# Query blocks of the token mixers as a sixth Strassen group, with adding transfers in the mixers and at the heads of the FFNs

## The chip, the cores and the metric

The kernel runs on one core of one Trainium2 chip. The metric is the device time of one execution in microseconds (us); the median of several executions is compared. Engines are named as the profile names them: PE (TensorE, matmuls), DVE (VectorE), ACT (ScalarE), POOL (GpSimd) and SP (SyncE, which here only issues transfers).

## The reference

One block of a streaming encoder on a sequence of 256 frames of width 2048, all in float32:

```
x = x + 0.5 * ffn(rmsnorm(x, g1), w1g, w1u, w1d)        # ffn: (silu(x@wg) * (x@wu)) @ wd, width 5632
h = rmsnorm(x, gm)
q_a, k_a, v_a, q_r, k_r, v_r, g_r, gate_a, gate_r = split(h @ w_in)
branch_a = chunked_band_attention(q_a, k_a, v_a, rel_bias) @ w_out_att
branch_r = (silu(g_r) * retention(rotary(q_r), rotary(k_r), v_r)) @ w_out_ret
x = x + (sigmoid(gate_a) * branch_a + sigmoid(gate_r) * branch_r) @ w_out
x = x + 0.5 * ffn(rmsnorm(x, g2), w2g, w2u, w2d)
out = rmsnorm(x, gf)
```

Each of q_a, k_a, v_a, q_r, k_r, v_r and g_r is 1024 columns wide (8 heads of 128), gate_a and gate_r are 2048 wide each.

## The kernel before, in words

**Products.** A float32 product is made of three faster ones (`three`, L137 to L145): ACT rounds a weight tile to its high part (L131), DVE subtracts to get the low part (L132), and PE multiplies high by high, low activations by high weights, and high by low. A weight tile holds 256 rows by 512 columns, 512 KB.

**Steps.** All work on PE is a list of steps that the Python code lays out before anything is issued. A *standard step* (L147) multiplies one weight tile by both halves of the sequence: 12 matmuls. A *Strassen step* (L573) does 6. A Strassen group (class `Strassen`, L518) computes two blocks of 512 columns from two weight blocks with 7 products of half-size blocks instead of 8: 28 steps, where standard jobs take 2 x 8 standard steps. In return it makes sums of weight tiles. Its group number is in its tile names (z10, z392, z728: the index of its first step), followed in the name of a split tile by phase, pair and r or s.

**Phases of a group.** The weights come in four pairs of tiles, k (kept) and x. Phase 0 multiplies the k tiles (r steps) and the sums x+k (s steps); phase 1 multiplies a third block from the ring of raw tiles (r) and the sums x+third (s); phase 2 a fourth block (r) and x-k (s); phase 3 the x tiles once more, to which POOL has added a weight block by an adding transfer (L587, it issues after DVE's subtraction L586). The first sum x+k is made by DVE (`first`, L534) or, for the pairs named in `added`, by an adding transfer from SBUF to SBUF on POOL's queue (`add_on`, L547), issued `ADD_WAIT` = 6 steps after the load of x. If the k tile of an added pair is prepared before that transfer is issued, DVE does the sum after all (L594). The FFNs have `ADDED = (0, 1)`; the mixers have none.

**What sets the order.** `run` (L249) goes through the steps; before the products of step c it prepares the weight tiles up to four steps ahead (casts on ACT, subtractions on DVE), and runs whatever is due at step c (`later`, `at`). Each engine works its own instructions in that order. SP loads raw tiles into a ring of 5, as the ring comes free. POOL loads the k and x tiles (`loads`, L540) into a room of 8 (`KEPT`); the first group's loads are spread over the 8 steps ahead of it (L712), one a step, and the FFNs get room for 2 more (`EXTRA`) when the first group has ended (L730). POOL also runs the norms' roots, loads the relative bias and reads back the gates, and it too works in order: a transfer that waits for another to land holds up what stands behind it.

**Weaving.** `weave` (L688) first lays out `lead` standard steps, then all groups one after the other, and lets in standard steps between their parts by a credit that grows with `share`. A group of an FFN has 8 standard steps among its 28, one of the mixers 9.6 on average.

**The stages.** FFN1: one plain block of columns and ten groups. Mixers: the standard jobs QA, KA, VA (two blocks each) and the first block of VR are woven with five groups (the two gates, in four blocks each, and g_r), whose results ACT writes to DRAM (L1056). At step `mixed` the woven part ends. Then come VR's second block, the jobs QR and KR, the three output products, and FFN2. The attention's heads (L916) and the retention's run beside these jobs: head h starts 4 steps after `mixed` plus 4h (L978, L1213), its scores, softmax, transposes and values spread over 6 steps. The query and key blocks are turned by PE into tiles of the pool `act` (`to_transposed`, L845), which has 30 tiles of 512 KB, 16 of them taken by the normalized activations in the mixers.

**Start.** Nine matmuls on zeros (L1170, `WARM`) run before the first product, 6 and 3.

Of the kernel before, what the change touches and what calls it, by code (L numbers as in the profile page):

```python
# [8 lines left out]
F32 = mybir.dt.float32  # L9
# [6 lines left out]
P = 128  # L16
SEQ = 256
# [9 lines left out]
NB = 512  # L27
# [10 lines left out]
AHEAD = (2, 3)  # L38
HALF_K = D // P // 2
LEAD = (10, 8)  # L40
MIX_LEAD = 8
RET_WAIT = (14, 5)
HELD = 6

MIX_SHARE = (0.85,) * 4 + (1.0,) * 4 + (0.8,) + (0.4,) * 3 + (0.15,) * 4
SHARE = (0.75,) * 4 + (1.0,) * 4 + (0.0,) * 4 + (0.2,) * 4
ADDED = (0, 1)
ADD_WAIT = 6
# [1 line left out]
PASSES = ((10,),) + tuple((b,) for b in range(10))  # L50
GATE_WAIT = 16
SQUARES = 8
WARM = (6, 3)
TAIL_PARTS = ((0, slice(0, NB)), (1, slice(0, NB // 2)), (1, slice(NB // 2, NB)))


# [21 lines left out]
def block_kernel(ctx: ExitStack, tc: tile.TileContext, x, g1, w1g, w1u, w1d, gm, w_in, rel, woa, wor, wo,  # L78
# [439 lines left out]
    class Strassen:  # L518
# [3 lines left out]

        def __init__(self, norm, w1, col1, w2, col2, evict, added=()):
            self.added, self.summed = added, set()
            self.norm, self.w, self.col, self.evict = norm, (w1, w2), (col1, col2), evict
            self.x, self.kept, self.acc, self.wide = {}, {}, {}, {}
            self.name = f"z{len(steps)}"
# [12 lines left out]
        def loads(self):  # L540


            def go(tiles, i, jc):
                tiles[jc] = apool.tile([P, KC, NB], F32, tag="act", name=f"{self.name}{'kx'[i]}{jc}")
                nc.gpsimd.dma_start(tiles[jc], chunk(self.w[i], self.rows(0, jc), self.col[i]))

            def add_on(jc):  # L547
                if jc not in self.summed:
                    self.summed.add(jc)
                    nc.gpsimd.dma_start(self.x[jc], self.kept[jc], accum_op=ALU.add)  # L550

            def second(jc):
                go(self.x, 1, jc)
                if jc in self.added:
                    later(ADD_WAIT, lambda: add_on(jc))

            return [
                (lambda jc=jc: second(jc)) if i else (lambda jc=jc: go(self.kept, 0, jc))
                for jc in range(HALF_K // KC) for i in range(2)
            ]  # L560
# [12 lines left out]
        def step(self, phase, jc, of_sum):  # L573
            made = {}
            name = f"{self.name}{phase}{jc}{'rs'[of_sum]}"
            n = HALF_K // KC

            def load():
                made["raw"] = weights_tile(f"raw{name}")
                i = 2 - phase  # L580
                fetch(made["raw"], self.w[i], self.rows(1, jc), self.col[i])

            def third():

                x, k = self.x[jc], self.kept[jc]
                nc.vector.tensor_sub(k, x, k)  # L586
                nc.gpsimd.dma_start(x, chunk(self.w[0], self.rows(1, jc), self.col[0]), accum_op=ALU.add)  # L587

            def prep():
                x = self.x[jc]  # L590
                if not of_sum:
                    if phase == 0:
                        made["w"] = split(self.kept[jc], name)
                        if jc not in self.summed:  # L594
                            self.summed.add(jc)
                            self.first(jc)
                        return
                    raw = made.pop("raw")
                    made["w"] = split(raw, name)
                    if phase == 1:  # L600
                        nc.vector.tensor_add(x, x, raw)
                elif phase == 2:
                    made["w"] = split(self.kept.pop(jc), name)
                elif phase == 3:
                    made["w"] = split(self.x.pop(jc), name)
                else:
                    made["w"] = split(x, name)
                    if phase == 1:
                        third()

            bank, form, fresh, closing = {
# [4 lines left out]
            }[phase, of_sum]  # L616

            def products():
                hi, lo = made["w"]
                if fresh and jc == 0:  # L620
                    self.bank(bank)
                three([
                    (
                        self.acc[bank], self.norm.form(form, KC * jc + i), (hi[:, i, :], lo[:, i, :]),
                        fresh and jc == 0 and i == 0, closing and jc == n - 1 and i == KC - 1,
                    )
                    for i in range(KC)
                ], True)
# [59 lines left out]
    def weave(jobs, apart, groups, lead, share, start=None, extra=0):  # L688
# [17 lines left out]

        for _ in range(lead):
            next_standard()
        ends = []
        rate = (len(queue) - apart) / (len(groups) * sum(share))  # L710
        credit = 0.0
        first = max(len(steps) - 8, D // NB)  # L712
        for n, (b, make) in enumerate(groups.items()):
            group = make()
            loads = group.loads()
            if start is not None and n == 0:
                loads[0] = lambda load=loads[0]: [start(), load()]
            kept.extend((first + i if n == 0 else 0, fn) for i, fn in enumerate(loads))
            for i, part in enumerate(group.steps()):
                steps.extend(part)  # L720
                credit += rate * share[i]
                if i + 1 == len(share):
                    at_hand[b] = len(steps) + 7

                turn = i + 1 == 3 * (HALF_K // KC)
                if (turn or credit >= (0.2 if (i + 1) % (HALF_K // KC) == 0 else 0.6)) and next_standard():
                    credit -= 1
            ends.append(len(steps))
        if extra:
            due.setdefault(ends[0], []).append(lambda: room.update(kept=room["kept"] + extra))  # L730
            due.setdefault(ends[-1], []).append(lambda: room.update(kept=room["kept"] - extra))
        for job, k in queue:
            steps.append(standard(job, k))

# [103 lines left out]
    QA, KA, VA, QR, KR, VR, GR, GA, GG = 0, W, 2 * W, 3 * W, 4 * W, 5 * W, 6 * W, 7 * W, 7 * W + D  # L838
    scale = HD ** -0.5
    tposed, nat = {}, {}  # L840

    def heads_t(ts):
        return slice(ts * P, (ts + 1) * P)

    def to_transposed(key, b, srcs, steps):  # L845

        dst = act_tile(F32, f"{key}{b}T")
        tposed[key, b] = dst

        def go(t):  # L850
            ps = transpose4(srcs[t], f"{key}{b}p{t}").rearrange("p (i q) -> p i q", i=4)
            if t == 0:
                nc.scalar.copy(dst[:, :, heads_t(t)], ps)
            else:
                nc.vector.tensor_copy(dst[:, :, heads_t(t)], ps)

        for t in range(NT):
            later(steps[t], lambda t=t: go(t))

    def att_qk_done(key, b):  # L860
        def done(acc):
# [40 lines left out]
    def nat_done(key, b, func, after=None):  # L902
        def done(acc):
            dst = act_tile(F32, f"{key}{b}")
            nat[key, b] = dst.rearrange("p a q -> p (a q)").rearrange("p (t n) -> p t n", t=NT)
            for t in range(NT):
                nc.scalar.activation(nat[key, b][:, t, :], acc[t], func, scale=nm.scale(t))
            if after is not None:
                after()

        return done
# [63 lines left out]
    def all_attention():  # L975
        for h in range(HEADS):
            for s, stage in attention(h):
                later(2 + 4 * h + s, stage)  # L978

    def retention(b):  # L980

# [65 lines left out]
    def gates(col1, col2, func, dsts):  # L1047
# [7 lines left out]
                nc.scalar.activation(r, bank, func, scale=nm.scale(t))  # L1055
            nc.scalar.dma_start(dsts[side][:, t, :], r)  # L1056

        return Strassen(nm, w_in0, col1, w_in0, col2, evict)

    both = ("acc", "acc")  # L1060
    groups = {
        b: (lambda b=b: gates(GA + b * NB, GG + b * NB, AF.Sigmoid, merge_dram[b])) for b in range(D // NB)
    }
    groups["gr"] = lambda: gates(GR, GR + NB, AF.Silu, ret_dram)
    weave(
        [proj(QA + b * NB, att_qk_done("qa", b), both) for b in range(2)]
        + [proj(KA + b * NB, att_qk_done("ka", b), both) for b in range(2)]
        + [proj(VA + b * NB, nat_done("va", b, AF.Copy), both) for b in range(2)]
        + [proj(VR, nat_done("vr", 0, AF.Copy), both)],
        0, groups, MIX_LEAD, MIX_SHARE,  # L1070
    )
    mixed = len(steps)
    add([proj(VR + NB, nat_done("vr", 1, AF.Copy))])
    for b in range(2):
        add([proj(QR + b * NB, ret_qk_done("qr", b)), proj(KR + b * NB, ret_qk_done("kr", b, lambda b=b: retention(b)))])

# [133 lines left out]
    at(mix - 18, load_rel)  # L1210
    at(mix - 18, lambda: later(4, load_gain(gm, 1)))
    at(mixed - 4, set_bias)
    at(mixed + 2, all_attention)  # L1213
    at(merges[0][0] + 4, lambda: later(8, load_gain(g2, 2)))
    at(mixed + 16, load_ret_gates)
    at(mixed + 20, set_decay)
# [66 lines left out]
```

## Time and profile before

| | us |
|---|---|
| median of 3 runs | 2058.67 (2058.22 to 2059.67) |
| the profiled execution | 2059.72 |
| its span, first to last instruction | 2058.0 |
| PE busy | 2039.3 (99%) |
| DVE busy | 1769.2 (86%) |
| ACT busy | 1490.3 (72%) |
| POOL busy | 327.1 (16%) |

The stages in this span: FFN1 to about 697, the woven part of the mixers to 1045, the rest of the mixers to about 1350, FFN2 to the end. A timeline row gives the start, the duration, the engine, the line, the operation, and output <- inputs; what stands in brackets is the engine's idle time ahead of it and what ended that. A row of the transfers gives the queue that issued them, their count, their size and the time from issue to landing. In a row of windows stand the stretch, its length, the busy time of PE, PEld, DVE, ACT and POOL, the granted clock, the share of the transfer engines, and GB/s. A busy PE isn't proof of full pace, as its matmuls overlap; the distance of starts shows that.

### The profile page before, as it was taken

The page shows a single profiled execution, that of the slowest core. Times are in us where ns is not written, and L with a number is a line of the kernel's source. Part 1 is how long each engine was busy: PE and PEld are TensorE (multiplying, and loading weights), DVE is VectorE, ACT ScalarE, POOL GpSimd, SP SyncE. Part 2 cuts the span into 40 slices and gives each one's busy share as a digit, 9 for nine tenths or more (in the row PEclk, how much of TensorE's full clock was granted, in tenths as well). Part 3 has the DMA queues.
Part 4 walks back from the last instruction along what each step waited for, and adds up shares of the span by engine and source line. Part 5 has one row for each costly group of instructions (what it writes and reads, how often), then busy time and mean ns, then how long its engine had stood idle before and what let it go on. Part 6 is the DMA issues. An engine that isn't in the chain of part 4 may idle for free.

```text
span 2058.0 us, 26285 instructions
## 1 busy us (share of the span) xinstructions
PE 2039.3 (99%) x9208; PEld 1683.2 (82%) x9208; DVE 1769.2 (86%) x1840; ACT 1490.3 (72%) x1894; POOL 327.1 (16%) x382
## 2 busy tenths in 40 slices
PE   9999999999999999999999999999999999999998
PEld 7688888888888888888888888888788888888886
DVE  7999999999998799889966667569989999989996
ACT  7778887888788767776665434556788787888785
POOL 1221222211112110122100000011112221112200
PEclk9999999999999999999999999999999999999999
DMA  8888899888878677788775645576889988889973
GB/s 288 242 241 265 259 273 277 258 238 251 263 231 264 239 206 253 255 283 263 216 274 177 222 141 190 185 243 192 260 265 267 275 241 237 267 260 274 276 205 133
DMA packets 224629, 496.37 MB, mean 241 GB/s; under 512 B 15520, under 2 KB 16272, under 8 KB 224496
## 3 DMA queue, kind: packets, MB, share of 16 engines
q1 hardware_dynamic: 156736, 301.50, 43.6%
q0 software_dynamic: 64416, 187.35, 35.0%
q10 hardware_dynamic: 3344, 5.84, 0.8%
q8 instruction: 72, 1.18, 0.2%
q14 instruction: 61, 0.50, 0.1%
HBM read 466.84 MB, written 8.91 MB: 231 GB/s over the span
## 4 chain that ended last, share of the span: by engine, by line
PE 92%; DVE 2%; DMA 1%; ACT 1%; issue 1%; POOL 0%; DVEq 0%; POOLq 0%; ACTq 0%
PE acc L145 15%; PE acc L142 15%; PE acc L143 15%; DMA z728x<-in_ffn_w_gate_dram 1%; DMA z728x<-z728k 1%; DVE lo L132 1%; PE z765a L142 0%; PE z154a L142 0%; PE z226a L142 0%; PE z946a L143 0%; PE z873a L142 0%; PE z298a L143 0%; PE z118a L143 0%; PE z801a L145 0%; PE z982a L145 0%
## 5 line engine op out<-in xcount | busy, mean ns | idle before, releaser
L132 DVE TENSOR_TENSOR lo<-raw,hi 128x1024 fp32r<-128x1024 f32 x367 | 446.2, 1219 | 140.2 <-ACT hi L131 138.5
L131 ACT CAST hi<-raw 128x1024 fp32r<-128x1024 f32 x367 | 383.8, 1050 | 174.6 <-PE acc L143 137.9
L805 ACT ACTIVATE xall<-acc 128x512 f32<-128x512 f32 x160 | 94.3, 589 | 13.6 <-PE acc L145 9.7
L802 ACT ACTIVATE acc<-xall 128x512 f32<-128x512 f32 x160 | 95.8, 599 | 9.1 <-DVE f1g L769 4.9
L142 PE MATMUL acc<-hi,mgh 128*128 128x512 f32 x128 | 50.2, 392 | 0.0
L143 PE MATMUL acc<-hi,mgl 128*128 128x512 f32 x128 | 49.8, 389 | 0.0
L142 PE MATMUL acc<-hi,nma01h 128*128 128x512 f32 x96 | 38.7, 404 | 0.0
L142 PE MATMUL acc<-hi,nma00h 128*128 128x512 f32 x96 | 38.6, 402 | 0.0
L143 PE MATMUL acc<-hi,nma01l 128*128 128x512 f32 x96 | 37.5, 390 | 0.0
L143 PE MATMUL acc<-hi,nma00l 128*128 128x512 f32 x96 | 37.4, 390 | 0.0
L143 PE MATMUL acc<-hi,nma11l 128*128 128x512 f32 x96 | 37.4, 390 | 0.0
L142 PE MATMUL acc<-hi,nma10h 128*128 128x512 f32 x96 | 37.4, 390 | 0.0
L142 PE MATMUL acc<-hi,nma11h 128*128 128x512 f32 x96 | 37.4, 390 | 0.0
L143 PE MATMUL acc<-hi,nma10l 128*128 128x512 f32 x96 | 37.4, 390 | 0.0
L145 PE MATMUL acc<-lo,mgh 128*128 128x512 f32 x128 | 35.5, 389 | 0.0
L145 PE MATMUL acc<-lo,nma01h 128*128 128x512 f32 x96 | 29.6, 390 | 0.0
L145 PE MATMUL acc<-lo,nma11h 128*128 128x512 f32 x96 | 29.6, 389 | 0.0
L145 PE MATMUL acc<-lo,nma00h 128*128 128x512 f32 x96 | 29.6, 389 | 0.0
L145 PE MATMUL acc<-lo,nma10h 128*128 128x512 f32 x96 | 29.6, 389 | 0.0
L145 PEld LDWEIGHTS acc<-lo,mgh 128*128 128x128 f32 x128 | 24.0, 188 | 5.0
L143 PEld LDWEIGHTS acc<-hi,mgl 128*128 128x128 f32 x128 | 24.0, 188 | 4.9
L142 PEld LDWEIGHTS acc<-hi,mgh 128*128 128x128 f32 x128 | 24.0, 188 | 4.8
(6633 smaller groups left out, 7111.7 us busy)
## 6 DMA issues: line engine op xcount, KB each, us to landing
raw<-in_ffn_w_down_dram SPq DMA_DIRECT2D x176, 512.0 KB, 7.0
raw<-in_w_in_dram SPq DMA_DIRECT2D x96, 512.0 KB, 4.7
raw<-in_w_out_dram SPq DMA_DIRECT2D x32, 512.0 KB, 4.1
raw<-in_ffn_w_up_dram SPq DMA_DIRECT2D x16, 512.0 KB, 5.5
raw<-in_w_out_att_dram SPq DMA_DIRECT2D x16, 512.0 KB, 4.3
raw<-in_w_out_ret_dram SPq DMA_DIRECT2D x16, 512.0 KB, 4.3
raw<-in_ffn_w_gate_dram SPq DMA_DIRECT2D x15, 512.0 KB, 4.8
z392x<-in_w_in_dram POOLq DMA_DIRECT2D x8, 512.0 KB, 7.5
```

Of the source, the lines that this page charges most:

```text
L131: nc.scalar.copy(hi, raw)
L132: nc.vector.tensor_sub(lo, raw, hi.bitcast(F32))
L142: nc.tensor.matmul(acc, ahi, whi, start=first, stop=False, **more)
L143: nc.tensor.matmul(acc, alo, whi, start=False, stop=False, **more)
L145: nc.tensor.matmul(acc, ahi, wlo, start=False, stop=last, **more)
L802: nc.scalar.activation(acc, xs[t][:, cols], AF.Copy, scale=2.0)
L805: nc.scalar.activation(xs[t][:, cols], acc, AF.Copy, scale=0.5)
```

## The change

- The two query blocks QA leave the standard jobs and become the first Strassen group of the mixers, `qa`. VR's second block joins the woven jobs, so `mixed` is followed at once by QR. There are now six groups with 7 standard steps each, after a lead of 6.
- The mixers' groups get adding transfers for pairs 0 and 2, and room for 2 more k or x tiles. The first group of each woven stage (FFN1, mixers, FFN2) gets adding transfers for all four pairs, issued 2 steps after the load of x. An added pair's sum falls back to DVE only when its s step is prepared, not its r step.
- The 2 more tiles of room come in phase 1 of the first group, and are taken back when the last has ended.
- Query, key and value tiles of the attention are written to DRAM by ACT's queue as soon as they are made, and read back by POOL's near `mixed`: block 0 from 3 steps ahead of it, block 1 from 5 steps behind it.
- The heads start at steps 3, 6, 10, 13, 17, 20, 24 and 27 after `mixed`.
- One warm-up matmul less.

```diff
-MIX_LEAD = 8
+MIX_LEAD = 6
+MIX_ADDED = (0, 2)
+HEAD_AT = (3, 6, 10, 13, 17, 20, 24, 27)
-MIX_SHARE = (0.85,) * 4 + (1.0,) * 4 + (0.8,) + (0.4,) * 3 + (0.15,) * 4
+MIX_SHARE = (0.5,) * 4 + (1.0,) * 4 + (0.0,) * 4 + (0.2,) * 4
-WARM = (6, 3)
+WARM = (6, 2)
...
             self.added, self.summed = added, set()
+            self.add_wait = ADD_WAIT
...
-                    later(ADD_WAIT, lambda: add_on(jc))
+                    later(self.add_wait, lambda: add_on(jc))
...
                         made["w"] = split(self.kept[jc], name)
-                        if jc not in self.summed:
+                        if jc not in self.added:
                             self.summed.add(jc)
                             self.first(jc)
                         return
...
                 else:
+                    if phase == 0 and jc not in self.summed:
+                        self.summed.add(jc)
+                        self.first(jc)
                     made["w"] = split(x, name)
...
             group = make()
+            if n == 0 and group.added:
+                group.added, group.add_wait = tuple(range(HALF_K // KC)), 2
...
             for i, part in enumerate(group.steps()):
+                if i == HALF_K // KC + 2:
+                    seconds.append(len(steps))
...
-            due.setdefault(ends[0], []).append(lambda: room.update(kept=room["kept"] + extra))
-            due.setdefault(ends[-1], []).append(lambda: room.update(kept=room["kept"] - extra))
+            due.setdefault(seconds[0], []).append(lambda: room.update(kept=room["kept"] + extra))
+            due.setdefault(len(steps), []).append(lambda: room.update(kept=room["kept"] - extra))
...
+    to_dram = {key: [dram.tile([P, 4, SEQ], F32, name=f"{key}{b}d") for b in range(HEADS // 4)] for key in ("qa", "ka", "va")}
+
+    def put_away(table, key, b, tile):
+        nc.scalar.dma_start(to_dram[key][b], tile)
+        del table[key, b]
+
+    def bring_back(b):
+        for table, key in ((tposed, "qa"), (tposed, "ka"), (nat, "va")):
+            t = act_tile(F32, f"{key}{b}back")
+            nc.gpsimd.dma_start(t, to_dram[key][b])
+            table[key, b] = t if table is tposed else by_tokens(t)
...
+        if home is not None:
+            later(max(steps) + 1, lambda: put_away(tposed, key, b, dst))
...
-                later(2 + 4 * h + s, stage)
+                later(HEAD_AT[h] + s, stage)
...
-        return Strassen(nm, w_in0, col1, w_in0, col2, evict)
+        return Strassen(nm, w_in0, col1, w_in0, col2, evict, MIX_ADDED)
...
+    def queries():
+        srcs = [{}, {}]
+
+        def evict(t, side, r):
+            if side == 0:
+                bank, r = r, tmp_tile(f"qa0{t}", "gate", 2)
+                nc.scalar.activation(r, bank, AF.Copy, scale=nm.scale(t))
+            srcs[side][t] = r
+            if len(srcs[side]) == NT:
+                to_transposed("qa", side, srcs[side], (3, 3))
+
+        return Strassen(nm, w_in0, QA, w_in0, QA + NB, evict, MIX_ADDED)
+
+    groups = {"qa": queries, **groups}
     weave(
-        [proj(QA + b * NB, att_qk_done("qa", b), both) for b in range(2)]
-        + [proj(KA + b * NB, att_qk_done("ka", b), both) for b in range(2)]
+        [proj(KA + b * NB, att_qk_done("ka", b), both) for b in range(2)]
         + [proj(VA + b * NB, nat_done("va", b, AF.Copy), both) for b in range(2)]
-        + [proj(VR, nat_done("vr", 0, AF.Copy), both)],
-        0, groups, MIX_LEAD, MIX_SHARE,
+        + [proj(VR + b * NB, nat_done("vr", b, AF.Copy), both) for b in range(2)],
+        0, groups, MIX_LEAD, MIX_SHARE, None, EXTRA,
     )
     mixed = len(steps)
-    add([proj(VR + NB, nat_done("vr", 1, AF.Copy))])
...
-    at(mixed + 2, all_attention)
+    at(mixed - 3, lambda: bring_back(0))
+    at(mixed + 5, lambda: bring_back(1))
+    at(mixed, all_attention)
```

More of the change, by code (lines that the diff above doesn't have):

```diff
@@ L708, in weave @@
             next_standard()
-        ends = []
+        seconds = []
         rate = (len(queue) - apart) / (len(groups) * sum(share))
@@ L727, in weave @@
                     credit -= 1
-            ends.append(len(steps))
         if extra:
-            due.setdefault(ends[0], []).append(lambda: room.update(kept=room["kept"] + extra))
-            due.setdefault(ends[-1], []).append(lambda: room.update(kept=room["kept"] - extra))
+            due.setdefault(seconds[0], []).append(lambda: room.update(kept=room["kept"] + extra))
+            due.setdefault(len(steps), []).append(lambda: room.update(kept=room["kept"] - extra))
         for job, k in queue:
@@ L840, in block_kernel, with by_tokens @@
     tposed, nat = {}, {}
+    to_dram = {key: [dram.tile([P, 4, SEQ], F32, name=f"{key}{b}d") for b in range(HEADS // 4)] for key in ("qa", "ka", "va")}
[7 more added lines that the diff above has]
+            table[key, b] = t if table is tposed else by_tokens(t)
+    def by_tokens(t):
+        return t.rearrange("p a q -> p (a q)").rearrange("p (t n) -> p t n", t=NT)
     def heads_t(ts):
@@ L848, in to_transposed @@
         tposed[key, b] = dst
+        home = to_dram.get(key)
         def go(t):
@@ L904, in done @@
             dst = act_tile(F32, f"{key}{b}")
-            nat[key, b] = dst.rearrange("p a q -> p (a q)").rearrange("p (t n) -> p t n", t=NT)
+            nat[key, b] = by_tokens(dst)
             for t in range(NT):
                 nc.scalar.activation(nat[key, b][:, t, :], acc[t], func, scale=nm.scale(t))
+            if key in to_dram:
+                put_away(nat, key, b, dst)
             if after is not None:
```

## The prediction

> **What bounds the kernel now.** I read the page first, then TensorE's waits, then its timeline at the starts of the three stages, then the software queue.
>
> ```profile
> span 2058.0 us, 26285 instructions
> PE 2039.3 (99%) x9208; PEld 1683.2 (82%) x9208; DVE 1769.2 (86%) x1840; ACT 1490.3 (72%) x1894; POOL 327.1 (16%) x382
> ```
>
> The profiled execution took 2059.7 us: a span of 2058.0 and 1.7 around it. TensorE is busy for 99% of it, so a change can gain in two ways only: fewer matmuls, or fewer of the few waits that TensorE still has. Who ends those waits:
>
> ```profile
> PE z728c L142 <- ACT hiz72800s L131: 1.4, 1, 1.4
> PE z10c L145 <- DVE loz1003s L132: 1.2, 1, 1.2
> PE f2a0p L387 <- DVE z692c L785: 0.7, 1, 0.7
> PE kr0p L387 <- DVE attl L382: 0.6, 1, 0.6
> ```
>
> Two groups stand out: z10, the first Strassen group of FFN1, and z728, the second of FFN2. Nothing of the mixers' woven part is among the long ones. The pace of an undisturbed step comes from three neighbouring starts in the timeline of PE:
>
> ```profile
> 1427.55 0.39 PE L142 MATMUL z692a<-hiz69213s,n2s6h 128*128 128x512 f32 x1
> 1428.90 0.39 PE L142 MATMUL acc<-hi,n2a01h 128*128 128x512 f32 x1
> 1431.62 0.39 PE L142 MATMUL z692b<-hiz69220r,n2a01h 128*128 128x512 f32 x1
> ```
>
> A Strassen step (6 matmuls) takes 1.36 us and a standard step (12) 2.72, 0.227 a matmul. (The 0.39 of one matmul is its latency.) With these I can say what the two groups lose:
>
> ```profile
> 39.34 0.39 PE L142 MATMUL z10a<-hiz1000r,n1a00h 128*128 128x512 f32 x1
> 107.09 0.39 PE L142 MATMUL z46a<-hiz4600r,n1a00h 128*128 128x512 f32 x1
> 1451.56 0.39 PE L142 MATMUL z728a<-hiz72800r,n2a00h 128*128 128x512 f32 x1
> 1468.52 0.40 PE L142 MATMUL z728c<-hiz72802s,n2s5h 128*128 128x512 f32 x1
> ```
>
> z10 takes 107.09 - 39.34 = 67.75. In it lie 28 Strassen steps (38.1), 8 standard ones (21.8) and one set of eight transposes (some 0.9): 60.8. So about 7.0 is lost. From 1451.56 to 1468.52 are 16.96, with six Strassen steps, one standard step and eight transposes: 11.8. About 5.2 is lost.
>
> **The change, part by part.** *Query blocks as a Strassen group.* Two jobs of 8 standard steps go (16 x 2.72 = 43.5) and 28 Strassen steps come (28 x 1.36 = 38.1): **-5.4**, all of it on TensorE's path. The transposes of the queries stay. VR1 only moves into the woven part.
>
> *One warm-up matmul less.*
>
> ```profile
> 8.41 0.63 PE L142 MATMUL acc<-hi,n1a00h 128*128 128x512 f32 x1
> 8.84 0.63 PE L143 MATMUL acc<-hi,n1a00l 128*128 128x512 f32 x1
> ```
>
> Starts are still 0.43 apart here, at the slow clock. If the clock rises at a fixed time, one more real matmul is done before that, worth 0.23 later: **-0.2** (0 to -0.4).
>
> *FFN1's first group.* VectorE did all four first sums; now four adding transfers do.
>
> ```profile
> L534 DVE TENSOR_TENSOR z10x<-z10x,z10k 128x1024 f32<-128x1024 f32 x4 | 4.9, 1218 | 0.0
> 52.92 1.03 ACT L131 CAST hiz1003s<-z10x 128x1024 fp32r<-128x1024 f32 x1
> 55.46 1.22 DVE L132 TENSOR_TENSOR loz1003s<-z10x,hiz1003s 128x1024 fp32r<-128x1024 f32 x1
> ```
>
> VectorE is freed of 4.9 us, and its lag behind ScalarE (55.46 against 52.92 + 1.03, some 1.5) is what TensorE waits for. But the sums now come from GpSimd's queue. Its prices:
>
> ```profile
> 21.27 0.91 POOL L545 DMA_DIRECT2D z10k<-in_ffn_w_up_dram  x1
> 26.51 0.74 POOL L545 DMA_DIRECT2D z10x<-in_ffn_w_gate_dram  x1
> z10k<-in_ffn_w_up_dram POOLq DMA_DIRECT2D x1, 512.0 KB, 7.2
> z10x<-in_ffn_w_gate_dram POOLq DMA_DIRECT2D x1, 512.0 KB, 16.5
> 1434.13 1.18 POOL L545 DMA_DIRECT2D z728x<-in_ffn_w_gate_dram  x1
> z728x<-in_ffn_w_gate_dram POOLq DMA_DIRECT2D x1, 512.0 KB, 17.5
> 1443.96 0.93 POOL L550 DMA_DIRECT2D z728x<-z728k  x1 [8.64 <-DMA z728x<-in_ffn_w_gate_dram]
> z728x<-z728k POOLq DMA_DIRECT2D x1, 512.0 KB, 10.7
> z82x<-z82k POOLq DMA_DIRECT2D x1, 512.0 KB, 5.3
> ```
>
> The first of the eight loads lands at 28.5, the eighth at 43.0: 2.07 each, one after the other. An adding transfer behind other work lands 3.0 after its predecessor (1454.7 against 1451.6); one that finds the queue empty takes 5.3. GpSimd will issue k0 x0 k1 x1, sum 0, k2 x2, sum 1, k3 x3, sum 2, sum 3. Each sum waits on GpSimd for its x, and the later loads are queued behind it. If all eight loads and four sums go at 2.07 and 3.0, the last sum lands at 26.4 + 16.6 + 12.0 = 55.0 or a little later; if the last two pairs go faster, because the raw weights' queue is quiet in phase 0, x3 lands near 47.5 and the last sum near 53.3. ScalarE's cast of it is now at 52.92, so at 53.3 the low part is ready near 55.5 and not at 56.7: 1.2 earlier. At 55.0 it is ready at 57.3, later than now, and phase 1 starts some 0.6 to 1.0 later. Behind that, VectorE works through phase 1 as before: its sums and differences are not touched, so the later losses of z10 stay. I take **-1.2** (bounds -3.0 and +1.0), nearer to the quick end, as few raw weights are due there.
>
> *FFN2's second group.* Its loads start only at 1430.48, since room for two more tiles came at the end of group one:
>
> ```profile
> 1430.48 1.21 POOL L545 DMA_DIRECT2D z728k<-in_ffn_w_up_dram  x1
> 1454.77 1.04 ACT L131 CAST hiz72800s<-z728x 128x1024 fp32r<-128x1024 f32 x1 [3.14 <-DMA z728x<-z728k]
> ```
>
> The room now comes in phase 1 of group one, so the first pair is there long before. The second pair takes the first one's place in the queue, and its sum lands by 1454.7; without the stall its cast is due at about 1456.5. What stays is the transposes of f2a0p, which wait for VectorE (0.7 and the restart, about 1.2): **-4.0** (bounds -2.5 and -5.2). FFN2's own first group shows no wait now; four sums cost it nothing by the same queue order, and up to 1.0 if they are late.
>
> The Trainium skill (SBUF — State Buffer, section "SBUF: two separate sides") says that a transfer issued from GpSimd cannot get its descriptors written while VectorE holds the shared port in a two-port mode. The rows speak against it here: from 1430.48 to 1434.13 GpSimd issued six loads, 0.73 apart, in a stretch in which VectorE is loaded like the rest of FFN2.
>
> *The mixers' first group.*
>
> ```profile
> 702.47 0.75 POOL L545 DMA_DIRECT2D z392k<-in_w_in_dram  x1
> z392k<-in_w_in_dram POOLq DMA_DIRECT2D x1, 512.0 KB, 4.6
> 720.49 0.39 PE L142 MATMUL z392a<-hiz39200r,nma00h 128*128 128x512 f32 x1
> ```
>
> With a lead of 6 it starts two standard steps sooner, at 715.0, and its loads two steps sooner; k0 and x0 pass ahead of the norm's root on GpSimd. From k1 (landing at 702.5 + 4.6 = 707.1) five loads and four sums follow: 707.1 + 10.4 + 9.2 to 12.0 = 726.7 to 729.5. The last sum's cast is due by 726: seven Strassen steps and one standard step after 715.0 are 727.2, less the cast. **+1.0** (bounds 0 and +3.0).
>
> *The mixers' steady part.*
>
> ```profile
> 92.00:98.00 6.00, 5.45 (x22) 4.08 (x23) 5.50 (x6) 6.00 (x7) 1.07 (x2) 1.00 1.04 391
> 240.00:301.00 61.00, 61.00 (x275) 50.59 (x274) 56.77 (x53) 49.46 (x61) 12.51 (x14) 1.00 0.91 263
> 855.00:920.00 65.00, 65.00 (x292) 53.64 (x291) 57.69 (x52) 43.85 (x49) 10.66 (x12) 1.00 0.82 254
> ```
>
> A group has 28 Strassen and 7 standard steps, 57.1 us, where 9.6 standard steps made it 64.2. VectorE has 57.69 in 65 now, so 57.0 a group; less two sums and 2.6 splits at 1.22 leaves 51.4 of 57.1, 90%. FFN1 runs at 56.77 of 61, 93%, without waits. Transfers: 29 of 0.52 MB, four gate tiles of 0.26 and one tile put away make 16.8 MB in 57.1 us, 294 GB/s; the queues reach 391. The put-away waits of ScalarE for VectorE's copy hold back casts that run three steps ahead. **+0.5** (bounds 0 and +3.0).
>
> *Attention.*
>
> ```profile
> 1018.95 2.02 POOL L349 DMA_DIRECT2D biasT<-rel_ext  x2
> biasT<-rel_ext POOLq DMA_DIRECT2D x2, 512.0 KB, 13.4
> 1045.29 0.60 PE L360 MATMUL psb<-id_sb,biasT 128*128 128x128 f32 x4
> ```
>
> GpSimd issues the bias right after the last group's last third-block transfer, 26.3 before the mixers' end; in the new order 12 Strassen and 2 standard steps lie there, 21.8. The bias lands 13.4 later, three returned tiles 6.2 after it: 2 us before the end, and the first head comes three standard steps (8.2) beyond it. So 10 us cover the return; without them TensorE would wait for the tiles directly. Heads follow each other in 3.5 steps instead of 4, between transposes that already wait once (0.6): **+0.5** (bounds -0.6 and +3.0, five such waits).
>
> Sum: -5.4 - 0.2 - 1.2 - 4.0 + 1.0 + 0.5 + 0.5 = **-8.8**, or 2050.9 against the profiled execution. The median of the runs, 2058.67, lies 1.0 below that execution, so the forecast is **2049.9**. All ends together are -14.6 (2044.1) and +2.1 (2060.8).
>
> **The rivals.** *Late sums at the heads.* All adding transfers cost 3.0 and more: z10 +1.0, FFN2's first group +1.0, its second only -2.5, the mixers' head +3.0. With -5.4 and -0.2 that is -3.1 and, with the two half microseconds, -2.1: about 2056.6. For it: every busy-queue sum I could price took 3.0. Against: the loads of phase 0 meet few raw weights. [...]
>
> *More gain.* With VectorE freed at its start, z10 loses nothing further and z728's stall goes whole: -5.4 - 0.2 - 7.0 - 5.2 = -17.8, or 2040.9. Against: VectorE is unbroken through z10's phase 1, where nothing is taken away.
>
> *The sums aren't done by transfers.* Where the sum's step is prepared before its transfer is issued, VectorE does it after all. Then z10 and the mixers' head stay as now: -8.6, beside the forecast. In the order as worked out the transfers come three steps ahead, so I hold it unlikely.
>
> *Slower: raw weights late in the mixers.*
>
> ```profile
> raw<-in_w_in_dram SPq DMA_DIRECT2D x5, 512.0 KB, 16.4
> ```
>
> This is SP's queue at 761 to 772, while eight loads pass on GpSimd's. Five buffers at one raw tile per 2.72 us cover 13.6, and with fewer standard steps and two adding transfers a group, TensorE could wait 16.4 - 13.6 = 2.8 in each of five group changes: +14.0, so 2063.9. It decides as soon as a raw tile lands more than 13.6 after TensorE could have used its buffer. Against: with 16.4 TensorE shows no such wait today, and the FFNs carry the same pattern at 263 GB/s.
>
> **How the numbers follow.** Forecast 0.62, late sums 0.15, more gain 0.08, sums by VectorE 0.03, slower 0.06; the last 0.06 is a wait of 3 to 6 in the attention (2053 to 2056). The range 2044 to 2057 holds the forecast's bounds nearly whole, the late sums and the attention. A measurement tells 0.2% from no change, 4.1 us: under 2054.6 is faster, over 2062.8 slower. Faster takes the forecast but 0.04, the gain, 0.03, and 0.09 of the late sums and the attention: 0.78. Slower is the raw weights, 0.06. The same: 0.16.
>
> **What would show it.** Right: 9183 matmuls, no wait at z728c, z10 near 66.5, no wait of the first head, the woven part without long waits. Wrong: a wait of TensorE or ScalarE on a z10x or qa sum, a head waiting for returned tiles, or casts in the mixers that wait for raw weights while TensorE stands.

## The result and the profile after

| us | before | after |
|---|---|---|
| median of 5 runs | 2058.64 (2058.06 to 2059.67) | 2078.34 (2075.20 to 2080.23) |
| span of the profiled execution | 2058.0 | 2078.5 |
| matmuls | 9208 | 9183 |

The ratio is 1.0091 (95% interval 1.0080 to 1.0103): by it the change makes the kernel about 19 us slower (the medians differ by 19.7), where the prediction had 9 us faster. The first lines of the page:

```profile
span 2078.5 us, 26358 instructions
PE 2043.8 (98%) x9183; PEld 1680.6 (81%) x9183; DVE 1773.0 (85%) x1844; ACT 1498.9 (72%) x1908; POOL 360.8 (17%) x422
```

The 24 matmuls of the queries and the one of the warm-up are gone, as forecast, and still PE's busy time is 4.5 longer than before (2039.3): some of the matmuls must have run slower. Next TensorE's waits after the change (engine, line, what it waited for; total, times, longest):

```profile
PE z425c L144 <- ACT hiz42502s L133: 4.7, 1, 4.7
PE z740c L144 <- ACT hiz74001s L133: 3.0, 1, 3.0
PE z530c L144 <- ACT hiz53002s L133: 2.7, 1, 2.7
PE z390c L144 <- ACT hiz39002s L133: 2.2, 1, 2.2
PE z495c L144 <- ACT hiz49502s L133: 1.5, 1, 1.5
...
PE z10c L144 <- ACT hiz1003s L133: 1.3, 1, 1.3
...
PE z390c L144 <- ACT hiz39003s L133: 0.9, 1, 0.9
...
PE z460c L144 <- ACT hiz46002s L133: 0.8, 1, 0.8
```

Before the change no group of the mixers stood in this list. Now five of the six do (z390 is the group of the queries), each at the cast of the same tile: phase 0, pair 2 (pairs count from 0, so this is the third), sum. That sum, x+k, is made by an adding transfer since the change. FFN2's second group, z740, waits in the same way for its second pair's sum, and z10 for its fourth. The sixth group, z565, has no group behind it whose loads could stand ahead of its sum, and it has no wait.

Where the third sum stays is seen on GpSimd's queue, here for group z460 (start, duration, operation):

```profile
828.62 1.17 POOL L548 DMA_DIRECT2D z460x<-in_w_in_dram  x1
829.98 0.73 POOL L548 DMA_DIRECT2D z460k<-in_w_in_dram  x1 [0.19 <-issue]
832.91 0.72 POOL L548 DMA_DIRECT2D z460x<-in_w_in_dram  x1 [2.20 <-DVE loz42521s L134]
837.14 0.72 POOL L548 DMA_DIRECT2D z495k<-in_w_in_dram  x1 [3.51 <-DVE loz42522s L134]
838.28 0.72 POOL L548 DMA_DIRECT2D z495x<-in_w_in_dram  x1 [0.41 <-DVE loz42523s L134]
846.18 0.92 POOL L553 DMA_DIRECT2D z460x<-z460k  x1 [7.17 <-DMA z460x<-in_w_in_dram]
```

The first row loads the x of the third pair, right behind its k. The sum (L553) may be issued only when this x has landed (the releaser in its brackets). By then four more loads stand in the queue: the fourth pair and the first pair of the *next* group. From the rows of the transfers, issue to landing of the third x, of the next group's x, and of the sum:

```profile
z460x<-in_w_in_dram POOLq DMA_DIRECT2D x1, 512.0 KB, 17.0
...
z495x<-in_w_in_dram POOLq DMA_DIRECT2D x1, 512.0 KB, 16.9
...
z460x<-z460k POOLq DMA_DIRECT2D x1, 512.0 KB, 12.3
```

So 828.62 + 17.0 = 845.6, 838.28 + 16.9 = 855.2 and 846.18 + 12.3 = 858.5: the sum lands 3.3 behind the last load of a tile that nobody needs for 50 us. ScalarE's cast follows at once, and TensorE has waited. The longest wait, at z425, comes about in the same way: its third sum, issued at 786.35 behind the first loads of z460, lands 11.5 later. The cast for z460:

```profile
858.61 1.04 ACT L133 CAST hiz46002s<-z460x 128x1024 fp32r<-128x1024 f32 x1 [5.75 <-DMA z460x<-z460k]
```

A long wait costs more than its length. The starts of matmuls after the one at z425:

```profile
799.00 0.50 PE L144 MATMUL z425c<-hiz42502s,nms5h 128*128 128x512 f32 x1 [4.72 <-ACT hiz42502s L133]
...
799.57 0.63 PE L144 MATMUL z425c<-hiz42502s,nms5h 128*128 128x512 f32 x1
800.00 0.63 PE L145 MATMUL z425c<-hiz42502s,nms5l 128*128 128x512 f32 x1
800.42 0.63 PE L147 MATMUL z425c<-loz42502s,nms5h 128*128 128x512 f32 x1
...
803.45 0.40 PE L144 MATMUL acc<-hi,nma01h 128*128 128x512 f32 x1
803.68 0.39 PE L145 MATMUL acc<-hi,nma01l 128*128 128x512 f32 x1
```

From 799.57 to 803.45 the starts are 0.43 apart instead of 0.23. Windows behind z390's waits (2.2, then 0.9), z460's (0.8) and z530's (2.7) show the granted clock, the third number from the end:

```profile
733.30:738.00 4.70, 4.70 (x12) 3.64 (x12) 3.69 (x5) 3.75 (x6) 0.00 (x0) 0.50 0.22 44
...
860.40:864.00 3.60, 3.53 (x16) 2.60 (x15) 3.60 (x4) 3.60 (x6) 0.00 (x0) 1.00 0.03 6
980.50:984.00 3.50, 3.50 (x10) 2.69 (x9) 3.50 (x4) 3.50 (x5) 0.00 (x0) 0.52 0.03 6
```

Some 30 matmuls in the mixers run at half the clock, 0.2 each, about 6 us. They count as busy, which is why PE's busy time grew.

The sum over the whole span, from the distances of PE's starts above their undisturbed pace: the woven part of the mixers loses 23.5 where it lost 1.6 (+21.9, 13.8 of it in delayed starts at sums, 6 in slow matmuls); z10 +2.4, FFN2's first two groups +1.9, the attention and retention -0.1, the rest -0.4; 24 matmuls less, -5.4. Together +20.3, and the spans differ by 20.5.

### The profile page after: what moved, and what is told of

Read it like the earlier page. It is cut to its first block, busy times and chain, and to the rows that moved or that the text cites. A ratio compares the mean times of both kernels' runs of the same rounds, so it can differ in the third digit from the quotient of the medians.

```text
span 2078.5 us, 26358 instructions
## 1 busy us (share of the span) xinstructions
PE 2043.8 (98%) x9183; PEld 1680.6 (81%) x9183; DVE 1773.0 (85%) x1844; ACT 1498.9 (72%) x1908; POOL 360.8 (17%) x422
## 5 line engine op out<-in xcount | busy, mean ns | idle before, releaser
L134 DVE TENSOR_TENSOR lo<-raw,hi 128x1024 fp32r<-128x1024 f32 x351 | 427.6, 1222 | 123.2 <-ACT hi L133 121.6
L133 ACT CAST hi<-raw 128x1024 fp32r<-128x1024 f32 x351 | 367.0, 1049 | 157.5 <-PE acc L145 124.5
L144 PE MATMUL acc<-hi,nma00h 128*128 128x512 f32 x80 | 32.3, 404 | 0.0
L144 PE MATMUL acc<-hi,nma11h 128*128 128x512 f32 x80 | 31.2, 391 | 0.0
L145 PE MATMUL acc<-hi,nma11l 128*128 128x512 f32 x80 | 31.2, 390 | 0.0
L144 PE MATMUL acc<-hi,nma10h 128*128 128x512 f32 x80 | 31.2, 390 | 0.0
L145 PE MATMUL acc<-hi,nma00l 128*128 128x512 f32 x80 | 31.2, 390 | 0.0
L145 PE MATMUL acc<-hi,nma10l 128*128 128x512 f32 x80 | 31.2, 390 | 0.0
L144 PE MATMUL acc<-hi,atth 128*128 128x512 f32 x64 | 26.2, 410 | 0.0
L144 PE MATMUL acc<-hi,reth 128*128 128x512 f32 x64 | 25.3, 395 | 0.0
```

The lines of the kernel that those rows point to most:

```text
L133: nc.scalar.copy(hi, raw)
L134: nc.vector.tensor_sub(lo, raw, hi.bitcast(F32))
L144: nc.tensor.matmul(acc, ahi, whi, start=first, stop=False, **more)
L145: nc.tensor.matmul(acc, alo, whi, start=False, stop=False, **more)
```

## The experiments

Theory 1: the adding transfers land late because of their place in GpSimd's queue. Rivals: the woven part is short of VectorE, and the waits only change their name (theory 2); or the sheer traffic of the adding transfers counts, wherever they stand. In the experiments the kernel before was run again beside each of them and had medians of 2059.8 to 2059.9, against 2058.6 above; each ratio below is to that.

**The sums taken from the transfers.** First for the five gate groups alone, then for the queries too:

```diff
-        return Strassen(nm, w_in0, col1, w_in0, col2, evict, MIX_ADDED)
+        return Strassen(nm, w_in0, col1, w_in0, col2, evict)
```

> The five gate groups of the mixers give all their first sums back to VectorE; the query group keeps its four adding transfers. Theory 1 (the sum of pair three stands on GpSimd's queue behind the loads of the next group, lands late, and each wait is followed by matmuls at the slow clock): the losses at z425, z460, z495 and z530, 7.0 + 1.4 + 2.1 + 4.5 = some 15 us, go, the loss at z390 stays: about 2063. Theory 2 (the woven part is short of VectorE, which has 52.7 of 60 us there and gets ten sums of 1.22 back): the waits change their name, from a sum's cast to a low part of VectorE, and the time stays above 2070.

Measured: 2064.56 (ratio to before 1.0021, 1.0012 to 1.0030). As theory 1 had it, within 2 us. The starts of groups z460 and z565, three groups apart:

```profile
841.33 0.39 PE L144 MATMUL z460a<-hiz46000r,nma00h 128*128 128x512 f32 x1
...
1012.69 0.39 PE L144 MATMUL z565a<-hiz56500r,nma00h 128*128 128x512 f32 x1
```

171.36, or 57.12 a group: the 57.1 that the prediction worked out for a group without any loss. With the adding transfers the same stretch took 180.27:

```profile
847.88 0.39 PE L144 MATMUL z460a<-hiz46000r,nma00h 128*128 128x512 f32 x1
...
1028.15 0.39 PE L144 MATMUL z565a<-hiz56500r,nma00h 128*128 128x512 f32 x1
```

```diff
-MIX_ADDED = (0, 2)
+MIX_ADDED = ()
```

> No adding transfer for first sums anywhere in the mixers, the query group's head included. Theory 1: the loss at z390 (about 7) goes as well, about 2057. Theory 2: VectorE is late at the head of the query group, where it also splits the norm, and the time is 2068 or more.

Measured: 2062.26 (1.0013, 1.0004 to 1.0023), between the 2057 of theory 1 and the 2068 of theory 2. At the head of the query group the loss falls from about 7 to 4.4 only; TensorE now waits there for VectorE's low part of the third sum, 1.2, and for phase 1. So at the head, and only there, theory 2 has a part. The windows of the woven part (PE, PEld, DVE, ACT, POOL busy, clock, share of the transfer engines, GB/s) of the kernel before, of the changed one and of this one:

```profile
720.00:1040.00 320.00, 320.00 (x1428) 265.03 (x1428) 289.73 (x262) 224.25 (x244) 49.03 (x54) 1.00 0.81 250
```

```profile
720.00:1040.00 320.00, 307.10 (x1330) 249.33 (x1330) 278.10 (x253) 215.26 (x239) 63.89 (x72) 0.98 0.90 270
```

```profile
720.00:1040.00 320.00, 316.82 (x1405) 259.76 (x1404) 306.94 (x280) 225.50 (x249) 55.80 (x62) 1.00 0.83 258
```

VectorE is busy for 306.9 of 320 here and TensorE stands for 3.2; in the changed kernel VectorE is busy for 278.1 and TensorE stands for 12.9. The eased engine was not the one that set the pace.

**The sums left to transfers, with another place in the queue.** First pairs one and two instead of one and three, then the pairs of the change with the issue moved:

```diff
-MIX_ADDED = (0, 2)
+MIX_ADDED = (0, 1)
```

> Pairs one and two are added by transfer in the mixers, as in the FFNs, instead of pairs one and three: as many transfers, but the second pair's sum is issued ahead of the next group's first loads. Theory 1: the sum lands about 3 us after the fourth pair (850.3 + 3 in the group at 848), just when it is needed: losses of at most 1 a group, about 2064 to 2067. Theory 2, or a third one by which the sheer traffic of the adding transfers counts and not their place: 2074 or more, as with pairs one and three.

Measured: 2076.86 (1.0079, 1.0062 to 1.0096). This is 10 above what theory 1 gave and inside the 2074 or more of both rivals. Groups z460, z495 and z530 lose 5.9 together (their lengths less 57.12 each) where they had lost 8.9, so about 2 each, twice the most that theory 1 allowed a group; TensorE now waits there mostly for low parts of VectorE. z390 and z425 stay slow. By its time this run fits the rivals better; what separates the theories is the next one.

```diff
+            if group.norm.name == "nm":
+                group.add_wait = 2
             loads = group.loads()
```

> Pairs one and three as in the change, but the sums are issued 2 steps after the load of x and not 6, so ahead of the next group's first loads. Theory 1: the third sum lands at about 853 and not at 858.5 in the group at 848, the waits of the four later groups go, the loss at z390 (already with 2 steps) stays: about 2063. The theory of sheer traffic: unchanged, 2074 or more. Against both: GpSimd now stands still for a landing ahead of the fourth pair's load, which may be late in turn.

Measured: 2071.47 (1.0056, 1.0041 to 1.0071). The total is 8 above what theory 1 gave and 2.5 below the 2074 of sheer traffic. Of the four later groups whose waits were to go, z460, z495 and z530 bear theory 1 out, and z425 doesn't. GpSimd's queue for z460, and the landing of its sum:

```profile
832.18 0.84 POOL L548 DMA_DIRECT2D z460k<-in_w_in_dram  x1
847.03 0.92 POOL L553 DMA_DIRECT2D z460x<-z460k  x1 [14.01 <-issue]
847.63 1.06 POOL L548 DMA_DIRECT2D z460x<-in_w_in_dram  x1
848.34 1.09 POOL L548 DMA_DIRECT2D z495k<-in_w_in_dram  x1
```

```profile
z460x<-z460k POOLq DMA_DIRECT2D x1, 512.0 KB, 7.3
```

The sum now stands ahead of three of the four loads, lands at 854.3 instead of 858.5 although the group starts 2.5 later, and this takes the wait away:

```profile
850.37 0.39 PE L144 MATMUL z460a<-hiz46000r,nma00h 128*128 128x512 f32 x1
...
1021.73 0.39 PE L144 MATMUL z565a<-hiz56500r,nma00h 128*128 128x512 f32 x1
```

171.36 again, without any loss, with the same number of adding transfers as in the changed kernel. That rules sheer traffic out for these three groups: the place in the queue decides. The price appears in z425, where GpSimd stands still for a landing and the fourth pair's x (issued at 789.61) lands at 798.2:

```profile
789.02 0.93 POOL L553 DMA_DIRECT2D z425x<-z425k  x1 [13.09 <-DMA z425x<-in_w_in_dram]
789.61 1.07 POOL L548 DMA_DIRECT2D z425x<-in_w_in_dram  x1
```

```profile
798.22 1.23 DVE L537 TENSOR_TENSOR z425x<-z425x,z425k 128x1024 f32<-128x1024 f32 x1 [4.47 <-DMA z425x<-in_w_in_dram]
...
799.97 1.22 DVE L134 TENSOR_TENSOR loz42502s<-z425x,hiz42502s 128x1024 fp32r<-128x1024 f32 x1
```

VectorE makes the fourth pair's sum itself, so it waits for that x, and the low part of the third sum, long since there, stands behind it in order: TensorE waits 2.9 and then runs slow. It is the same queue with another victim: z425 takes 66.90 here, where it took 65.64 in the changed kernel.

**The FFNs' part alone**, on the kernel before: first the four adding transfers of the first groups, then the earlier room (ffn_room).

```diff
...
             group = make()
+            if n == 0 and group.added:
+                group.added, group.add_wait = tuple(range(HALF_K // KC)), 2
```

> The kernel before with one part of the change: the first group of each FFN gets four adding transfers, issued 2 steps after the load of x; room, mixers and warm-up as before. By the prediction's term (-1.2) 2058.6 beside 2059.8 for the kernel before. By the trace of the changed kernel, where the fourth sum of z10 is 1.3 us late and phase 1 and 2 lose what they lost before: +1 to +2.5, so 2061 to 2062.

Measured: 2060.61 (1.0006, 0.9996 to 1.0015): no difference from the kernel before that can be told, and not the gain that the prediction's term gave; z10 takes 68.94 against 67.75, +1.2.

```diff
+                if i == HALF_K // KC + 2:
+                    seconds.append(len(steps))
...
-            due.setdefault(ends[0], []).append(lambda: room.update(kept=room["kept"] + extra))
+            due.setdefault(seconds[0], []).append(lambda: room.update(kept=room["kept"] + extra))
```

> The kernel before with another part alone: the 2 more tiles of room of the FFNs come in phase 1 of the first group and are taken back when the last has ended. By the prediction's term (-4.0) 2055.8. By theory 1 the first sum of FFN2's second group comes in time, but the sum of its second pair stands behind four loads and lands some 3 us after the last of them: its stall replaces the other and the group loses 6 to 7.5 instead of 5.2, 2060 to 2062.

Measured: 2060.57 (1.0008, 0.9999 to 1.0018). No gain. Its largest wait of TensorE, and GpSimd's queue behind it:

```profile
PE z728c L142 <- ACT hiz72801s L131: 3.6, 1, 3.6
```

```profile
1441.61 0.93 POOL L550 DMA_DIRECT2D z728x<-z728k  x1 [7.94 <-DMA z728x<-in_ffn_w_gate_dram]
1442.20 1.07 POOL L545 DMA_DIRECT2D z728k<-in_ffn_w_up_dram  x1
1442.93 1.08 POOL L545 DMA_DIRECT2D z728x<-in_ffn_w_gate_dram  x1
1443.65 1.08 POOL L545 DMA_DIRECT2D z728k<-in_ffn_w_up_dram  x1
1444.37 1.08 POOL L545 DMA_DIRECT2D z728x<-in_ffn_w_gate_dram  x1
1449.53 0.92 POOL L550 DMA_DIRECT2D z728x<-z728k  x1 [4.08 <-DMA z728x<-in_ffn_w_gate_dram]
```

The first sum is early enough now, and the wait for it gone. But the second one is again issued behind four loads. If that is the cause, it should go when VectorE makes this one sum (ffn_one_sum):

```diff
+            if n == 1 and group.added:
+                group.added = (0,)
```

> The kernel before with the earlier room of the FFNs, as in ffn_room, but in the second group of each FFN only the first pair is added by transfer; VectorE makes the second pair's sum. Theory 1 (the second pair's sum lands 3 us behind four loads that were issued ahead of it, and its wait is followed by slow matmuls): the loss of 3.7 and some 2 of slow clock behind it go, the group loses about 2.0 instead of 7.5, so 2055 to 2056 beside 2059.8 and 2060.6. A rival: VectorE, busy for over 90%, makes this sum no earlier, and its low part takes the place of the wait: 2059 or more.

Measured: 2057.18 (0.9988, 0.9979 to 0.9997). Right in the mechanism: the wait of 3.6 is gone, and the group's length from its first matmul to the next group's falls from 71.61 to 67.29 (68.74 before the change). The gain of 3.4 against the kernel with the room alone is a little less than expected, since TensorE waits for two low parts of VectorE (0.7 and 0.6) instead: the rival has that much of a part.

**The query group alone**: the changed kernel with the FFNs as before and every sum of the mixers made by VectorE, once with the change's lead (called qa_lead6 below) and once with the old one (qa_lead8).

```diff
-MIX_ADDED = (0, 2)
+MIX_ADDED = ()
...
-            if n == 0 and group.added:
-                group.added, group.add_wait = tuple(range(HALF_K // KC)), 2
...
+            due.setdefault(seconds[0] if group.norm.name == "nm" else ends[0], []).append(lambda: room.update(kept=room["kept"] + extra))
```

> The changed kernel with the FFNs as before (two added pairs, room at the end of the first group) and all sums of the mixers on VectorE; what is left is the query group, its lead of 6, the tiles put away and brought back, the order of the heads, the earlier room in the mixers. The 24 matmuls fewer are worth -5.4. Theory 1 with the trace of the kernel without adding transfers in the mixers: the query group's head loses 4.4, its turned tiles 1.2, so nearly all is eaten: 2058 to 2060. If VectorE is not late at the head: 2055.

Measured: 2059.31 (1.0000, 0.9991 to 1.0009), as expected: the 24 matmuls are worth their 5.4, and the head gives them back (z390 about 4.4, the queries' transposes 1.1).

```diff
-MIX_LEAD = 6
+MIX_LEAD = 8
```

> The same with a lead of 8 standard steps, as before the change. If the loss at the head comes from starting 5.4 us earlier than VectorE has split the norm and the weights of the lead, the 4.4 at the head shrinks to under 1: 2055. If it comes from the group itself, as with a lead of 6: 2058 to 2060.

Measured: 2060.30 (1.0003, 0.9993 to 1.0012). Half right: the head's loss does shrink to 1.2, but the gain is lost further on. The transposes lose 2.2, two low parts of VectorE at 864 and 988 are late, and the groups have fewer standard steps between them. So two standard steps moved to the front take 3.2 off the head's loss, and about as much is lost behind it.

**Mended versions.** First, as qa_lead8_adds, with a lead of 8 adding transfers only from the third group of the mixers on, 2 steps after the load. The FFNs keep their room as before the change, and VectorE makes all sums of their first groups, as it did there:

```diff
+            if n == 0 or n == 1 and not apart:
+                group.added = ()
+            elif not apart:
+                group.add_wait = 2
...
```

> As qa_lead8, but from the third group of the mixers on pairs one and three are added by transfer, issued 2 steps after the load of x; in the first two groups VectorE makes all sums. If VectorE's share (306 of 320 us in the woven part) is what is left of the loss with a lead of 8 (low parts late by 0.6 to 0.8 at 864 and 988), these go: 2058. If the transfers cost as much as VectorE gains, 2060 as with qa_lead8.

Measured: 2059.70 (1.0002, 0.9993 to 1.0010). That fits the 2060 and not the 2058. The low parts at 864 and 988 are as late as without the adding transfers (0.8 each, against 0.6 and 0.8), although VectorE is busy for 157.2 of the 170 us from 840 on and not for 163.5, so its share in that stretch is not their cause. What is remains open.

And with the FFNs of the kernel with one sum (all_mended):

```diff
                 group.added = ()
+            elif n == 1:
+                group.added = (0,)
             elif not apart:
                 group.add_wait = 2
...
```

> qa_lead8_adds with the FFNs of ffn_one_sum (VectorE's sums in the first group, the first pair only in the second, early room). If both theories hold, the two gains add: 2058 - 4 = 2054. If either fails, 2056 to 2060.

Measured: 2055.80 (0.9981, 0.9972 to 0.9990), the lowest median of all: 4.1 under the kernel before, between the 2054 expected if both theories hold and the 2056 if one fails. Most of it comes from FFN2, whose second group takes 66.43 and not 68.74. Its page:

```profile
PE 2033.5 (99%) x9183; PEld 1676.3 (82%) x9183; DVE 1789.5 (87%) x1860; ACT 1501.3 (73%) x1908; POOL 346.2 (17%) x406
```

PE's busy time is 5.8 below that of the kernel before: the 25 matmuls make 5.7 of it, and behind none of its waits does the clock fall.

```diff
-                to_transposed("qa", side, srcs[side], (3, 3))
+                to_transposed("qa", side, srcs[side], (3, 6))
```

> all_mended with the two transposes of each query block 3 steps apart instead of at one step, so that the second does not wait for VectorE's copy of the first's bank (1.1 to 2.2 us at 785 in the kernels with a query group): 1 to 2 less than all_mended. If the wait is for VectorE's place in order and not for the bank, the same as all_mended.

Measured: 2057.34 (0.9988, 0.9979 to 0.9997): not better. The queries' wait is gone, and the transposes of the next keys wait instead, 2.3 for ScalarE's copy of the bank.

## Why the prediction was wrong, point by point

- *The query blocks* (-5.4): right as a count, 9183 matmuls. With VectorE making the sums, the head of the group gave the time back (the query group alone, above).
- *The mixers' steady part* (+0.5, bounds 0 and +3.0): this is the step that failed: the groups from z425 on lost some 15. The step compared averages, VectorE 90% and 294 GB/s of 391, and both were fine: without adding transfers a group takes exactly the 57.1 of the prediction. What it left out was to follow one third-pair sum through GpSimd's queue, as it had done for the heads. Its price of 3.0 behind a predecessor was right (3.3 here); the predecessor was not asked for. With the earlier room this is the next group's first pair, and the sum lands 12.3 after its issue.
- *What a wait costs* was counted at its length. Behind most waits of 1.7 us and more the clock halves for 3.4 to 6.8 us, some 2 us more for each, and no term of the sum had that. The Trainium skill (TensorE: Matmul & The Clock Gate, section "HAM oscillation — how this bites in real kernels") sets the limit at idle gaps of about 3.4 us. In these traces gaps of 2.7 at z530, of 2.2 at z390 (the clock falls at 731.3, ahead of the second wait, which starts at 731.9) and of 1.8 at z425 of the kernel with pairs one and two were enough. A gap of 1.5 (z495) was not. A rule of 3.4 would have put the slow clock in the mixers of the changed kernel only behind z425's wait. The length alone doesn't decide. With the query group alone TensorE waits for the first pair's sum of z740 for 1.7 in both kernels. Behind it the clock halves with a lead of 8 and does not with a lead of 6 (the row of the wait, the same in both, then a window behind it in each, the lead of 8 first):

```profile
PE z740c L144 <- ACT hiz74000s L133: 1.7, 1, 1.7
```

```profile
1457.70:1461.10 3.40, 3.40 (x10) 2.29 (x9) 3.40 (x5) 0.27 (x2) 0.00 (x0) 0.50 1.03 331
```

```profile
1455.50:1462.00 6.50, 5.25 (x22) 3.29 (x23) 5.83 (x7) 3.45 (x5) 0.00 (x0) 1.00 0.90 277
```

  Nor did the 2.3 ahead of the keys' transposes in the last kernel bring it. What else decides is not shown.
- *The mixers' first group* (+1.0, at most +3.0): about 7. The fourth sum was put at 726.7 to 729.5, needed by 726. It landed at 731.6, and its cast let TensorE go on at 732.8; the third, landing at 728.5, had held TensorE up before. The three later sums land 3.1 behind the transfer ahead of them, as priced; the first lands 5.6 behind the load ahead of it. That is not the whole loss: with VectorE making the sums 4.4 is still lost there, at VectorE's own low parts (the query group alone), and with a lead of 8 besides only 1.2. So a good part of the 7 goes with the start two standard steps sooner, at which VectorE is late too, and the term had followed GpSimd's queue alone.
- *FFN1's first group* (-1.2, bounds -3.0 and +1.0): +1.2 alone, +2.4 in the changed kernel (where the other 1.2 comes from was not followed). The fourth sum was put at 53.3 to 55.0. Its issue in the changed kernel, and its time to landing:

```profile
50.46 0.87 POOL L553 DMA_DIRECT2D z10x<-z10k  x1 [5.73 <-DMA z10x<-in_ffn_w_gate_dram]
```

```profile
z10x<-z10k POOLq DMA_DIRECT2D x1, 512.0 KB, 5.7
```

  It lands at 56.1: its x has landed only just before 50.46, and by then only the third sum, which lands at 52.2, is left in the queue. So the sum costs about the 5.3 of an empty queue (5.7 here), not 3.0. That price stood in the prediction and was not used for this sum. The rival of late sums had this place right, with +1.0.
- *FFN2's second group* (-4.0): +1.2, and with its first group +1.9. The first half of the step was right: the wait for the first pair's sum goes. That the second pair's "sum lands by 1454.7" fell, as the four loads behind the first sum go out at once when that sum is issued, ahead of the second. With that one sum back on VectorE the room is worth 2.7.
- *The attention* (+0.5): -0.1, with no wait for a returned tile. Right.
- *The warm-up* (-0.2): can't be told. The first products wait for the norm's first tiles, and the landing of its gain moves the start by more than that from one execution to the next.
- *The rivals.* The late sums were meant for the heads alone and gave 2056.6. The slower side came, but not by its mechanism: raw tiles took up to 21 us to land, and TensorE waited for none. The six issues 0.73 apart that the prediction held against the port rule don't test it: they show when GpSimd issued and not when the transfers were made ready, and no row shows the mode in which VectorE worked.
- *The range* (2044 to 2057) ended below the sum of the terms' own upper ends, 2060.8, which left out the up to 1.0 of FFN2's first group. The 2078.34 lies beyond both.

## What to carry to other kernels

A transfer that computes is not free work taken from a busy engine: it moves the step into an in-order queue, where it waits for its operands to land, holds up what is queued behind it, and lands behind all that was issued ahead of it. Before work goes to such a queue, follow one item through it, issue by issue, in the steady state too, and name the load in front of it; a share of the bandwidth or of an engine's time doesn't show this. Where the queue also fetches ahead for the next block, each sum must stand ahead of that prefetch, or stay on the engine that has it now, and a wait of TensorE of about 1.7 us or more is to be priced with the slow matmuls that may stand behind it.

## What the runs showed of the hardware

- An adding transfer of 512 KB from SBUF to SBUF lands 4.6 to 6.4 after its issue where it finds the queue empty (median 4.9 in the changed kernel). Behind other transfers it lands 2.3 to 5.6 after the one ahead of it (median 3.1). A load behind others takes about 2.1.
- Landings on GpSimd's queue keep the order of issue in every trace. The Trainium skill (DMA: Bandwidth & Descriptors, section "Two DMAs through the same engine are not ordered") says that within one queue of one engine descriptors start in order, and it doesn't promise that they end so. The rows, which show landings, agree: the sum of z460 lands 12.3 after its issue, behind the four loads.
- The clock's fall behind waits of 1.7 to 3 us, with its numbers above, was not expected.
